# A two-layer hybrid decoder trunk: the order of output blocks and token chunks in three residual products, and how long their weights are kept

## The chip, the cores and the metric

The kernel runs on one core of one Trainium2 chip. The metric is the time of one execution on the device, in microseconds, and less is better. The engines are called as in the profile: PE multiplies matrices (PEld is its weight load), DVE, ACT and POOL are the three engines for elementwise work, and SP issues most of the transfers.

## What is computed

One inference step of two layers with 1024 features, for a prompt of 16 meta tokens and 512 tokens and for eight samples of 8 tokens, 592 tokens in all:

```
layer 0:  x = LN(a*x + W_out @ [stick-breaking attention | multi-scale pooling])
          x = LN(a*x + W_down @ (gelu(conv3(W_g x)) * (W_v x)))
layer 1:  x = LN(a*x + W_out @ (gelu(W_gate x) * RG-LRU(conv4(W_rec x))))
          x = LN(a*x + W_down @ (gelu(conv3(W_g x)) * (W_v x)))
```

a is the fourth root of 4, the FFN has 2816 hidden features, and RG-LRU is a gated linear recurrence along the tokens. LN takes the mean and the variance over the 1024 features of a token. The outputs are y without the meta tokens, and the caches (keys, values, pooling, convolution and recurrence states).

## The kernel before, in words

Features lie on the 128 partitions, tokens along the free dimension; 1024 features are eight blocks of 128. The tokens are cut into two chunks, chunk 0 (0 to 295) and chunk 1 (296 to 591). In the second half of layer 1 chunk 0 leaves out the first 14 tokens and has 282 columns.

**Products.** Every product is done in a split form of fp32. `split` (L100, L101) makes a high half on ACT and a low half, the difference, on DVE or POOL, and `mm3` (L127) then does three matmuls for each block of 128 inputs: high weight by high operand, high weight by low operand, low weight by high operand. `weights` loads one output block's weights over SP's queue into `wraw` and splits them into `whl`. `wraw` has two buffers, the split weights have six in layer 1 and in both FFNs (two pools in turn).

**Residual products.** The class `Residual` does a product whose result is added to the residual x (`r0_m` is block m of x for chunk 0, `r1_m` that for chunk 1) and the LayerNorm behind it. There are four: the attention's output, the last group of layer 0's FFN (6 input blocks, from about 731 us), the output of the recurrent layer (5 input blocks), and the last group of layer 1's FFN (6 input blocks, the end of the kernel). `mms(0)` does the eight output blocks of chunk 0 in the order 0 to 7, and keeps the weights of the last `keep` (3) blocks; then `second` does chunk 1 in the order 7 to 0 with `mms(1)`, which loads the weights of the other five again. Behind each block `post` adds it to x (L201), subtracts a first estimate of the mean (L209; the tile `s0` or `s1`, taken from the first block of that chunk at L206 to L207) and adds x and its square on POOL to the sums S1 (L219; a copy, L211, for the first block) and S2 (L220); "post" stands below for L201 and L209. The sums' tiles are `S10` and `S20` for chunk 0, `S11` and `S21` for chunk 1. `stats` lets PE sum S1 and S2 over the partitions with a matrix of ones (L228, tiles `mu` and `q2`), and takes the root of the variance on ACT (L232) with one refining step on DVE (L234 to L236). `norm` then centres each block (L250), scales it (L251), adds the bias (L252) and makes the high half `xh` on ACT (L257) and the low half `xl` on POOL (L258): the operands of the next stage. At the end of the kernel there is no next stage; the blocks go out, and POOL does four of chunk 1's eight normalisations and leaves two of its sums to PE.

**What sets the order.** The statistics and norms of a chunk are not done at once but put into a list, `pend`, and taken from it by `pop` between later pieces of PE work: those of chunk 0 while chunk 1's blocks are done, those of chunk 1 during the first blocks of the next stage. Each is given a high priority (`urgent`), so that the scheduler puts it ahead of other work on its engine. Each engine then works through its own list in order.

```
            for k, _ in enumerate(self.mms(1)):
                if k == 0:
                    self.pop()
                elif k >= 2:
                    self.pop(1 if k < 12 else 2)
```

**The next stages.** Layer 1 begins with five blocks on chunk 0 (three of the recurrent branch, tile `prc`, and two of the gate branch, `pgt`, 120 matmuls), then those blocks on chunk 1. A finished recurrent block goes through the convolution `conv4` (L937 and following, DVE), whose result is split (`ch`, `cl`) for the gate matrices (`pga`, L961) of the recurrence. An FFN begins with six blocks of W_g (tile `pg`) on chunk 0 and then on chunk 1.

## Time and profile before

| | |
|---|---|
| time, three executions | 1468.46, 1469.25, 1470.31 us (median 1469.25) |
| the profiled execution | 1470.56 us, span of the core 1468.8 us |
| PE busy | 1371.5 us, 93% of the span |
| DVE, ACT, POOL busy | 56%, 40%, 31% |
| chain of work that ended last | PE 75%, DVE 14%, issue 4%, ACT 3%, POOL 2% |
| weights loaded for the three products | 26 blocks of 384 KB (both FFNs), 13 of 320 KB (recurrent output) |

A row of the profile in order of time begins with the start and the length in us; x8 says that it stands for eight instructions in a row. What stands in brackets at its end is the idle time of that engine just before, and what ended it. A row of a group has the busy time in us and the mean ns of one instruction behind the bar.

### The profile page before, as it was taken

How to read it: one execution, taken by the hardware profiler on the slowest of the kernel's cores; microseconds unless marked ns; L12 is line 12 of the kernel's file. 1: busy time of each engine (PE TensorE's matmuls, PEld its weight loads, DVE VectorE, ACT ScalarE, POOL GpSimd, SP SyncE). 2: the span in 40 equal slices, each digit the busy share in tenths (PEclk: the TensorE clock that was granted, in tenths of full speed). 3: DMA queues.
4: the chain of work that ended last, by engine and by line, in shares of the span. 5: the costliest groups of instructions: out<-in, count | busy, mean ns of one | idle time of the engine just before them, and what ended most of it. 6: DMA issues, size and time to landing. Idle time of an engine off the chain costs nothing.

```text
span 1468.8 us, 26738 instructions
## 1 busy us (share of the span) xinstructions
PE 1371.5 (93%) x10491; PEld 1294.3 (88%) x10491; DVE 816.1 (56%) x1220; ACT 587.3 (40%) x1083; POOL 451.2 (31%) x621
## 2 busy tenths in 40 slices
PE   8999798998999999999997787897999999999995
PEld 7988555798999999999997787886999999999994
DVE  4226676575743344334477699888734344433456
ACT  4333575444522233213245466735522133312333
POOL 3112220346320011102257656447531012101244
PEclk9999899999999999999998898998999999999997
DMA  9499887842422222222241210143222222222121
GB/s 311 169 373 372 308 286 259 302 135 87 129 73 87 86 73 87 79 80 79 67 120 58 62 65 28 28 121 115 73 91 82 87 81 78 87 87 87 57 90 65
DMA packets 78592, 183.74 MB, mean 125 GB/s; under 512 B 9458, under 2 KB 18291, under 8 KB 78467
## 3 DMA queue, kind: packets, MB, share of 16 engines
q1 hardware_dynamic: 75362, 170.77, 35.3%
q0 software_dynamic: 3104, 11.27, 2.1%
q8 instruction: 83, 1.36, 0.4%
q14 instruction: 43, 0.34, 0.1%
HBM read 176.38 MB, written 5.62 MB: 124 GB/s over the span
## 4 chain that ended last, share of the span: by engine, by line
PE 75%; DVE 14%; issue 4%; ACT 3%; POOL 2%; DMA 1%; SPq 0%; DVEq 0%; ACTq 0%; POOLq 0%
PE pv L127 19%; PE pg L127 18%; PE pdn L127 14%; PE pr L127 4%; PE pqk L127 3%; PE zs L640 2%; PE pv L415 2%; DVE r L251 2%; PE av L668 2%; DVE whl L101 2%; PE zp L517 1%; PE pu L127 1%; DVE r L250 1%; PE prc L127 1%; DVE r L209 1%
## 5 line engine op out<-in xcount | busy, mean ns | idle before, releaser
L100 ACT ACTIVATE whl<-wraw 128x1024 fp32r<-128x1024 f32 (+4 forms) x217 | 212.4, 981 | 338.9 <-PE pdn L127 150.6
L127 PE MATMUL pg<-xh,whl 128*128 128x296 f32 (+1 forms) x1408 | 293.0, 300 | 4.2 <-ACT xh L257 4.2
L101 DVE TENSOR_TENSOR whl<-wraw,whl 128x1024 fp32r<-128x1024 f32 (+3 forms) x198 | 234.9, 1187 | 102.2 <-ACT whl L100 101.6
L127 PE MATMUL pv<-xh,whl 128*128 128x296 f32 (+1 forms) x1408 | 290.2, 298 | 0.0
L127 PEld LDWEIGHTS pg<-xh,whl 128*128 128x128 f32 x1408 | 231.5, 191 | 4.8 <-ACT xh L257 4.4
L127 PEld LDWEIGHTS pv<-xh,whl 128*128 128x128 f32 x1408 | 229.0, 188 | 0.0
L127 PE MATMUL pg<-xl,whl 128*128 128x296 f32 (+1 forms) x704 | 210.7, 301 | 6.8 <-POOL xl L258 6.8
L127 PE MATMUL pv<-xl,whl 128*128 128x296 f32 (+1 forms) x704 | 209.1, 297 | 0.0
L127 PE MATMUL pdn<-fh,whl 128*128 128x296 f32 (+1 forms) x1024 | 207.7, 298 | 0.0
L101 POOL TENSOR_TENSOR fl<-f,fh 128x592 fp32r<-128x592 f32 (+1 forms) x44 | 82.7, 1879 | 273.1 <-ACT fh L100 273.1
L127 PEld LDWEIGHTS pdn<-fh,whl 128*128 128x128 f32 x1024 | 165.5, 188 | 0.0
L127 PE MATMUL pdn<-fl,whl 128*128 128x296 f32 (+1 forms) x512 | 151.7, 297 | 0.0
L127 PEld LDWEIGHTS pg<-xl,whl 128*128 128x128 f32 x704 | 133.8, 191 | 9.0 <-POOL xl L258 8.9
L127 PEld LDWEIGHTS pv<-xl,whl 128*128 128x128 f32 x704 | 133.0, 189 | 0.0
L807 DVE TENSOR_SCALAR gc<-ge,sm 128x608 f32<-128x608 f32 x44 | 26.2, 595 | 169.4 <-ACT ge L770 159.4
L801 POOL COPY fout<-ge 128x2 f32<-128x2 f32 x44 | 15.7, 358 | 326.1 <-ACT ge L767 326.0
L767 ACT ACTIVATE ge<-pg 128x296 f32<-128x296 f32 (+2 forms) x88 | 33.8, 386 | 157.2 <-PE pg L127 155.2
L127 PEld LDWEIGHTS pdn<-fl,whl 128*128 128x128 f32 x512 | 96.4, 189 | 0.0
L393 DVE TENSOR_TENSOR_SCAN kp<-kp,zero 128x256 f32<-128x256 f32 (+5 forms) x70 | 54.1, 774 | 73.7 <-ACT kp L392 73.2
L864 DVE SCALAR_TENSOR_TENSOR r<-r,pdn 128x296 f32<-128x296 f32 (+1 forms) x64 | 29.0, 459 | 118.0 <-PE pdn L127 118.0
L821 DVE TENSOR_TENSOR f<-gc,pv 128x296 f32<-128x296 f32 (+1 forms) x88 | 37.5, 426 | 99.6 <-PE pv L127 75.4
L127 PE MATMUL pr<-fh,whl 128*128 128x296 f32 (+1 forms) x384 | 79.4, 300 | 0.0
(263 smaller groups left out, 2726.9 us busy)
## 6 DMA issues: line engine op xcount, KB each, us to landing
ck<-in_ck SPq DMA_DIRECT2D x128, 256.0 KB, 5.1
cv<-in_cv SPq DMA_DIRECT2D x128, 256.0 KB, 5.2
wraw<-in_w_g SPq DMA_DIRECT2D x44, 512.0 KB, 3.3
wraw<-in_w_vv SPq DMA_DIRECT2D x44, 512.0 KB, 3.4
wraw<-in_w_d SPq DMA_DIRECT2D x32, 512.0 KB, 3.3
wraw<-in_w_d SPq DMA_DIRECT2D x26, 384.0 KB, 3.1
wraw<-in_w_lo SPq DMA_DIRECT2D x13, 320.0 KB, 3.0
wraw<-in_w_o POOLq DMA_DIRECT2D x8, 512.0 KB, 6.4
```

What stands on the lines that cost most here:

```text
L100: act.activation(h, src, AF.Copy)
L101: (le or dve).tensor_tensor(l, src, h.bitcast(F32), op=OP.subtract)
L127: pe.matmul(ps, lhsT=w[:, wi, s], rhs=x[k][:, lo:hi], start=(n == 0), stop=(n == 3 * nk - 1))
L251: dve.scalar_tensor_tensor(x, x, g, rs, op0=OP.mult, op1=OP.mult)
L393: dve.tensor_tensor_scan(kp[:, n - 1::-1], kp[:, n - 1::-1], zero.to_broadcast([128, n]), 1.0 if carry is None else carry, op0=OP.mult, op ...
L415: pe.matmul(p, lhsT=x[k][:, i * 128:i * 128 + n], rhs=w[k // 4][:, wi, s], start=(j == 0), stop=(j == 3 * KB - 1))
L640: pe.matmul(z[c * 32:c * 32 + 32, :256].rearrange("p (j n) -> p j n", j=2), lhsT=qb[b][:, c, r, :], rhs=kt[:, b, :, c * 128:c * 128 + 128] ...
L668: pe.matmul(av[c * 32:c * 32 + 32], lhsT=an[:, j * 128 + c * 32:j * 128 + c * 32 + 32], rhs=vt[:, :, j, c * 128:c * 128 + 128], start=(u = ...
L767: act.activation(e[:, k + lo:k + z], p[:, :z - lo], AF.Copy)
L807: dve.tensor_scalar(t[:, :n], e[:, :n], cws[0], smc("fcb", L * FB + j), op0=OP.mult, op1=OP.add)
L821: dve.tensor_tensor(f[:, lo:z], t[:, lo:z], p[:, :z - lo], op=OP.mult)
L864: dve.scalar_tensor_tensor(x, x, ALPHA if gi == 0 else 1.0, p, op0=OP.mult, op1=OP.add)
```

## The change

Three of the four residual products no longer call `mms(0)` and `second`, but a new method `both(4)`. It does output blocks 0 to 3 for both chunks in turn (chunk 0, then chunk 1), then blocks 4 to 7 for chunk 0, then 7 to 4 for chunk 1. A block's weights are kept until both chunks have used them, so each is loaded and split once: 16 blocks of 384 KB instead of 26, and 8 of 320 KB instead of 13. The statistics and norms of chunk 0 are put on the list behind its last block and taken from it in eight steps between the halves of chunk 1's last four blocks (1, 1, 2, 2, 1, 1, 1, 1 entries); what is left goes to the next stage. The last lines of `mms` become a method `finish`, and the attention's product stays as it was.

```
--- before.py
+++ after.py
@@ -44,6 +44,7 @@
 STEP = 3.5
 HQ, EP = 19, 8
 PRO = 6
+JOINT = 4
 WINDOWS = (2, 4, 8, 16)
 CTX = 15
 BW = 3 + TP + NS * 11
@@ -187,6 +188,38 @@
                     prev()
                 prev = partial(self.post, ci, m, p, n)
                 yield 0.19 * nk, 0.09 * nk
+            self.finish(ci, prev)
+
+        def both(self, nj):
+            nk, ws, prev = self.nk, {}, None
+            seen = [0, 0]
+            seq = [(m, ci) for m in range(nj) for ci in range(2)] + [(m, 0) for m in range(nj, KB)]
+            seq += [(m, 1) for m in range(KB - 1, nj - 1, -1)]
+            late = deque()
+            for m, ci in seq:
+                lo, hi = self.chunks[ci]
+                if m not in ws:
+                    ws[m] = weights(self.wsrc[m], nk)
+                p = psum["d"]("pr")[:, :hi - lo]
+                for k in (0, nk // 2):
+                    mm3(p, ws[m], self.ih, self.il, lo, hi, nk, k, nk // 2 if k == 0 else nk)
+                    if seen[0] == KB:
+                        self.pop(late.popleft())
+                if prev is not None:
+                    prev()
+                prev = partial(self.post, ci, m, p, seen[ci])
+                seen[ci] += 1
+                if ci:
+                    del ws[m]
+                if (m, ci) == (KB - 1, 0):
+                    late.extend([1, 1, 2, 2] + [1] * (2 * (KB - nj) - 4))
+                    self.finish(0, prev)
+                    prev = None
+            self.finish(1, prev)
+
+        def finish(self, ci, prev):
             self.pend.append(prev)
             self.pend.append(partial(self.urgent, HPS, self.stats, ci))
             for m in range(KB):
@@ -865,9 +898,7 @@
             else:
                 sp.dma_start(O["ffn"][:, L], fout)
                 res = Residual(I[f"w_d{gi}"][L], nk, hh, hl, 1.0, 2 * L + 1, last, chunks)
-                for _ in res.mms(0):
-                    pass
-                res.second()
+                res.both(JOINT)
         return res
 
     res.second()
@@ -1044,9 +1075,7 @@
     a, b = LGROUPS[1]
     res = Residual(I["w_lo1"], b - a, [ys[i][0] for i in range(a, b)], [ys[i][1] for i in range(a, b)], 1.0, 2,
                    chunks=CH2)
-    for _ in res.mms(0):
-        pass
-    res.second()
+    res.both(JOINT)
     res = ffn(1, res, True)
     res.pop(99)
 
```

Lines behind the new code have other numbers: L128, L242, L252, L253, L284 and L290 of the changed kernel are L127, L209, L219, L220, L251 and L257 of the one before.

POOL, in layer 0's FFN product, from chunk 0's first sum on. Before (the tiles are chunk 0's sums `S10`, `S20`, its blocks `r0_m` and their squares `sq0`):

```order
L211 COPY S10_8418<-r0_0_78 128x296
L220 TENSOR_TENSOR S20_8419<-S20_8419,sq0_8452 128x296
L219 TENSOR_TENSOR S10_8418<-S10_8418,r0_1_79 128x296
L220 TENSOR_TENSOR S20_8419<-S20_8419,sq0_8482 128x296
L219 TENSOR_TENSOR S10_8418<-S10_8418,r0_2_80 128x296
L220 TENSOR_TENSOR S20_8419<-S20_8419,sq0_8512 128x296
```

and in the changed kernel, where `S11`, `S21`, `r1_m` and `sq1` are those of chunk 1:

```order
L244 COPY S10_8413<-r0_0_78 128x296
L244 COPY S11_8447<-r1_0_4146 128x296
L252 TENSOR_TENSOR S10_8413<-S10_8413,r0_1_79 128x296
L253 TENSOR_TENSOR S20_8414<-S20_8414,sq0_8476 128x296
L253 TENSOR_TENSOR S21_8448<-S21_8448,sq1_8506 128x296
L252 TENSOR_TENSOR S11_8447<-S11_8447,r1_1_4147 128x296
L252 TENSOR_TENSOR S10_8413<-S10_8413,r0_2_80 128x296
L253 TENSOR_TENSOR S20_8414<-S20_8414,sq0_8531 128x296
L252 TENSOR_TENSOR S11_8447<-S11_8447,r1_2_4148 128x296
```

Chunk 0's sums now take turns with chunk 1's, for the first four blocks of each.

DVE, from the last scaling of chunk 0 to the first centring of chunk 1, behind the same product. Before (`pr` is a block's product, `whl` the split weights of layer 1's first blocks, `s1` the mean of chunk 1):

```order
L251 SCALAR_TENSOR_TENSOR r0_7_85<-r0_7_85,sm_70,S10_8418 128x296
L201 SCALAR_TENSOR_TENSOR r1_1_4147<-r1_1_4147,pr_8848 128x296
L101 TENSOR_TENSOR whl_9091<-wraw_9090,whl_9091 128x1024
L201 SCALAR_TENSOR_TENSOR r1_0_4146<-r1_0_4146,pr_8878 128x296
L209 TENSOR_TENSOR r1_1_4147<-r1_1_4147,s1_8679 128x296
L101 TENSOR_TENSOR whl_9128<-wraw_9127,whl_9128 128x1024
L209 TENSOR_TENSOR r1_0_4146<-r1_0_4146,s1_8679 128x296
L250 TENSOR_TENSOR r1_0_4146<-r1_0_4146,s1_8679 128x296
```

and in the changed kernel:

```order
L284 SCALAR_TENSOR_TENSOR r0_6_84<-r0_6_84,sm_70,S10_8413 128x296
L284 SCALAR_TENSOR_TENSOR r0_7_85<-r0_7_85,sm_70,S10_8413 128x296
L283 TENSOR_TENSOR r1_0_4146<-r1_0_4146,s1_8446 128x296
L283 TENSOR_TENSOR r1_2_4148<-r1_2_4148,s1_8446 128x296
L283 TENSOR_TENSOR r1_1_4147<-r1_1_4147,s1_8446 128x296
L283 TENSOR_TENSOR r1_4_4150<-r1_4_4150,s1_8446 128x296
```

Chunk 1's last two posts and two weight splits now stand ahead of chunk 0's scalings, and the centring of chunk 1 follows the scalings directly.

ACT, the last high halves of chunk 0 (`xh5` to `xh7`) there, the mean of chunk 1 (L229, L230) and the root of its variance (L232). Before:

```order
L257 ACTIVATE xh5_8658<-r0_5_83 128x296
L100 ACTIVATE whl_9356<-wraw_9355 128x1024
L257 ACTIVATE xh6_8659<-r0_6_84 128x296
L257 ACTIVATE xh7_8660<-r0_7_85 128x296
L229 ACTIVATE S11_8680<-mu_8995 128x296
L230 ACTIVATE s1_8679<-mu_8995 128x296
L232 ACTIVATE S11_8680<-S21_8681 128x296
L767 ACTIVATE re0_8973<-prc_8942 128x296
L767 ACTIVATE re1_9024<-prc_8982 128x296
```

and in the changed kernel, where the root is L265 and the bias of chunk 1's first block is L285:

```order
L290 ACTIVATE xh3_8750<-r0_3_81 128x296
L290 ACTIVATE xh4_8751<-r0_4_82 128x296
L290 ACTIVATE xh5_8752<-r0_5_83 128x296
L265 ACTIVATE S11_8447<-S21_8448 128x296
L290 ACTIVATE xh6_8753<-r0_6_84 128x296
L290 ACTIVATE xh7_8754<-r0_7_85 128x296
L285 ACTIVATE r1_0_4146<-r1_0_4146,sm_70 128x296
```

The root of chunk 1 now stands ahead of the last two high halves of chunk 0.

PE, in layer 1, the first blocks on chunk 1 (`prc` with different numbers are different recurrent blocks, `pgt` is a gate block). Before:

```order
L127 MATMUL prc_9161<-xh0_8653,whl_8938 128x296
L127 MATMUL prc_9201<-xh0_8653,whl_8978 128x296
L127 MATMUL prc_9241<-xh0_8653,whl_9128 128x296
L127 MATMUL pgt_9281<-xh0_8653,whl_9039 128x296
L127 MATMUL prc_9161<-xl0_8661,whl_8938 128x296
L127 MATMUL prc_9161<-xh0_8653,whl_8938 128x296
L127 MATMUL prc_9201<-xl0_8661,whl_8978 128x296
L127 MATMUL prc_9201<-xh0_8653,whl_8978 128x296
```

and in the changed kernel, at the end of the first recurrent block and the begin of the second:

```order
L128 MATMUL prc_9136<-xh6_8753,whl_8913 128x296
L128 MATMUL prc_9136<-xh7_8754,whl_8913 128x296
L128 MATMUL prc_9136<-xl7_8762,whl_8913 128x296
L128 MATMUL prc_9136<-xh7_8754,whl_8913 128x296
L128 MATMUL prc_9176<-xh0_8747,whl_8953 128x296
L128 MATMUL prc_9176<-xl0_8755,whl_8953 128x296
L128 MATMUL prc_9176<-xh0_8747,whl_8953 128x296
```

Before, four blocks took turns at each operand; now a block goes through all eight operands before the next one begins.

## Rows read from the trace of the kernel before

**Rows 1.** The page's busy times, over the whole span.

```profile
PE 1371.5 (93%) x10491; PEld 1294.3 (88%) x10491; DVE 816.1 (56%) x1220; ACT 587.3 (40%) x1083; POOL 451.2 (31%) x621
```

**Rows 2.** Windows: busy time (and instructions) by engine, granted clock, DMA share, GB/s.

```profile
730.70:770.40 39.70, 38.52 (x275) 37.81 (x275) 28.27 (x50) 17.29 (x29) 20.06 (x18) 1.00 0.38 111
770.40:830.00 59.60, 43.88 (x265) 41.62 (x264) 43.91 (x51) 27.59 (x62) 43.71 (x42) 0.83 0.17 55
820.00:900.00 80.00, 61.55 (x393) 59.41 (x394) 75.64 (x66) 51.26 (x80) 49.90 (x43) 0.87 0.19 63
1009.00:1060.00 51.00, 44.16 (x302) 42.80 (x302) 40.97 (x55) 30.53 (x69) 36.88 (x38) 0.90 0.25 79
1445.00:1469.00 24.00, 6.29 (x12) 3.88 (x12) 12.76 (x22) 8.43 (x18) 9.82 (x11) 0.64 0.25 86
```

**Rows 3.** Waits of PE, 765 to 832 us: total, times, longest.

```profile
PE prc L127 <- ACT xh L257: 6.2, 2, 3.2
PE pga L961 <- ACT ch L100: 6.8, 1, 6.8
```

**Rows 4.** Groups by form on DVE, whole span: weight splits by width.

```profile
L101 DVE TENSOR_TENSOR whl<-wraw,whl 128x1024 fp32r<-128x1024 f32 x154 | 191.9, 1246 | 85.4 <-ACT whl L100 85.1
...
L101 DVE TENSOR_TENSOR whl<-wraw,whl 128x768 fp32r<-128x768 f32 x26 | 27.5, 1056 | 6.5 <-ACT whl L100 6.2
...
L101 DVE TENSOR_TENSOR whl<-wraw,whl 128x640 fp32r<-128x640 f32 x13 | 13.2, 1012 | 7.8 <-ACT whl L100 7.8
```

**Rows 5.** Groups by form on POOL, 740 to 760 us: the sums of chunk 0.

```profile
L219 POOL TENSOR_TENSOR S<-S,r 128x296 f32<-128x296 f32 x7 | 8.4, 1196 | 0.0
L220 POOL TENSOR_TENSOR S<-S,sq 128x296 f32<-128x296 f32 x7 | 7.5, 1077 | 0.9 <-ACT sq L215 0.9
```

**Rows 6.** POOL in order of time: the last sum of chunk 0 there.

```profile
757.42 1.52 POOL L219 TENSOR_TENSOR S<-S,r 128x296 f32<-128x296 f32 x1
```

**Rows 7.** PE in order of time: chunk 0's statistics, first and second chunk of layer 1.

```profile
758.99 0.77 PE L228 MATMUL mu<-S,ones 128*128 128x296 f32 x2 [1.18 <-POOL S L219]
...
776.62 0.62 PE L127 MATMUL prc<-xh,whl 128*128 128x296 f32 x1 [3.01 <-ACT xh L257]
...
803.06 1.06 PE L127 MATMUL prc<-xh,whl 128*128 128x296 f32 x3 [3.24 <-ACT xh L257]
...
824.86 1.36 PE L961 MATMUL pga<-ch,wga 128*128 128x296 f32 x4 [6.79 <-ACT ch L100]
```

**Rows 8.** DVE in order of time, from chunk 0's statistics to layer 1's first convolution.

```profile
760.75 3.10 DVE L250 TENSOR_TENSOR r<-r,s 128x296 f32<-128x296 f32 x8
...
773.59 8.07 DVE L251 SCALAR_TENSOR_TENSOR r<-r,sm,S 128x296 f32<-128x296 f32 x8
...
791.66 6.59 DVE L250 TENSOR_TENSOR r<-r,s 128x296 f32<-128x296 f32 x8 [5.34 <-ACT s L230]
...
800.71 4.72 DVE L251 SCALAR_TENSOR_TENSOR r<-r,sm,S 128x296 f32<-128x296 f32 x8
...
815.06 0.60 DVE L937 TENSOR_SCALAR rt<-re,sm 128x616 f32<-128x616 f32 x1 [9.63 <-ACT re L770]
```

**Rows 9.** ACT in order of time: the last two operands of chunk 0.

```profile
788.06 0.78 ACT L257 ACTIVATE xh<-r 128x296 fp32r<-128x296 f32 x2
```

**Rows 10.** The chain of waits behind the recurrent output product: start us, us, what.

```profile
1030.67 28.35 PE pg L127 x209
```

**Rows 11.** DVE in order of time, behind the recurrent output product.

```profile
1010.58 6.96 DVE L251 SCALAR_TENSOR_TENSOR r<-r,sm,S 128x282 f32<-128x282 f32 x8
```

**Rows 12.** POOL in order of time, same place.

```profile
1026.67 3.94 POOL L258 TENSOR_TENSOR xl<-r,xh 128x282 fp32r<-128x282 f32 x4
```

**Rows 13.** The end of the kernel, DVE in order of time.

```profile
1440.93 5.75 DVE L251 SCALAR_TENSOR_TENSOR r<-r,sm,S 128x282 f32<-128x282 f32 x8
...
1455.32 0.47 DVE L231 SCALAR_TENSOR_TENSOR S<-q,S 128x296 f32<-128x296 f32 x1 [6.15 <-PE q L228]
...
1460.05 0.47 DVE L236 SCALAR_TENSOR_TENSOR S<-sq,S 128x296 f32<-128x296 f32 x1
```

## The prediction

> **What bounds the kernel now.** I read the page's busy times first. TensorE (PE) is busy for 1371.5 of 1468.8 us [rows 1], so the kernel is PE's, and only what makes PE wait, or wait less, can move the end. The windows then say where it waits [rows 2]. The product of layer 0's FFN that this change reorders runs from 730.7 to 770.4 us with PE busy for 38.52 of 39.70 us: it is full, although it reloads five weights. The loss lies right behind the products: 43.88 busy of 59.60 us from 770.4, 44.16 of 51 us from 1009, and 6.29 of the last 24 us. There PE waits for normalised tokens, or the kernel for its last ones. Between 820 and 900 us it is another engine: VectorE (DVE) is busy for 75.64 of 80 us, PE for 61.55. The list of PE's waits behind layer 0's product names the operand h of the next stage, 6.2 us in two waits, and the gate matrices of layer 1, which wait 6.8 us for the first convolution's result [rows 3]. So the change is worth what it moves in the LayerNorms behind the three products, not what it saves in loading.
>
> **The reloads themselves: nothing directly.** Each product loads eight weights instead of thirteen. On DVE that takes away ten splits of 768 columns at 1.056 us and five of 640 at 1.012 us, 15.6 us in all [rows 4]; ScalarE (ACT) loses their high halves and SP's queue their loads, so that the next stage's weights come sooner; with a DMA share of 0.38 [rows 2] they were not late. Inside the products PE was full, so I cost this at 0. It counts only where DVE is behind.
>
> **Place 1, behind layer 0's FFN product.** Times are on the clock of the execution before.
>
> (a) Chunk 0's statistics come later. Its eighth block is now the twelfth on PE, and POOL sums the blocks of both chunks as they come. Ahead of chunk 0's last sum of x there stood one copy and 13 sums; now two copies and 18. Sums take 1.196 and 1.077 us [rows 5], 1.14 on the mean, so five more and a copy (taken as 0.6, half a sum) are 6.3 us. Before, the last sum ended at 757.42 + 1.52 = 758.94 us [rows 6] and the matmul for the mean followed at 758.99 [rows 7]; now it is ready at 765.2. In PE's order the matmul stands behind 251 of the product's 288; at 39.70/288 = 0.138 us each that is 730.7 + 34.6 = 765.3 us. The two meet, so PE hardly waits for it.
>
> (b) Chunk 0's normalising. From that matmul DVE needed 14.6 us before it began the eight scalings of L251 at 773.59 [rows 8]: 1.8 us until it could start and 12.8 us full of centring (L250), three weight splits, and posts of chunk 1. Now one split (1.25 us, [rows 4]) and five small operations at 0.47 us fewer stand there, which leaves 9.2 us; but POOL is still summing, and eight centrings then take up to 6.59 us instead of 3.10 [rows 8]. I take half of that 3.5 us more: 765.4 + 1.8 + 9.2 + 1.7 = 778 us, 4.5 us later than before.
>
> (c) Chunk 1 comes earlier. Before, four posts and two splits stood between the two chunks, then DVE waited 5.34 us for chunk 1's mean, because POOL was still summing. Now its sums are done when DVE gets there, and the centring follows at once: 778 + 8.07 + 6.59 = 792.7 us, and scaling 2.5 us after that (798.25 to 800.71 before), at 795.2 us instead of 800.71 [rows 8].
>
> (d) PE. ACT's order now has chunk 1's root ahead of the last two operands of chunk 0, so these come at about 794 us instead of 788.06 [rows 9], and their low halves by 795.5. Of the 120 matmuls on chunk 0, 55 stand behind the last of these: at 28.35/209 = 0.136 us, as in the row of the other transition [rows 10], they end at 803 us. Chunk 1 began at 803.06 [rows 7]: no gain for PE here. But chunk 1 is then ready as a whole, and PE does its first recurrent block at one go, 24 matmuls or 3.3 us, where it took turns between four blocks. DVE's first convolution can begin at about 806.5 instead of 815.06 us, where it stood idle for 9.63 us [rows 8]. The gate matmuls stand behind four such blocks, 803 + 13.1 = 816 instead of 824.86, with their operand long there. From here DVE bounds the layer [rows 2], and its work is the same. **Term 1: 8.5 us gained.** If only PE counted it would be 0; if POOL left DVE alone, see the third rival, 14.
>
> **Place 2, behind the recurrent output product.** The same pattern: by (a) and (b) chunk 0's scaling begins some 3.5 us later than 1010.58 and takes the same 6.96 us [rows 11], to 1021. POOL no longer has sums of chunk 1 between the low halves, which then follow each other: the last six, at 3.94/4 = 0.985 us, end at 1027.4 instead of 1030.6 us [rows 12]. From there PE was full [rows 10], and so it stays; PE's order has three matmuls more ahead of the last low half (77 instead of 74), 0.4 us. **Term 2: 3.2 + 0.4 = 3.6 us.** Ends: 0 and 7.
>
> **Place 3, the end.** DVE did chunk 0's eight scalings from 1440.93, 5.75 us, ahead of the last three blocks of chunk 1; so chunk 1's statistics reached it only at 1455.32 [rows 13]. Now the scalings begin some 6 us later, 1447, but chunk 1's last sums and products are all ahead of them. They end at 1452.7, and chunk 1's variance follows at once, 2.6 us earlier. From there the end is taken as the same; the second half of the centring, which falls on a DVE at work until 1460.05 [rows 13], may gain or lose a little. **Term 3: 2.6 us.** Ends: 0, if the scalings slip to 1449.6 and so end at 1455.3 as before, and 6, the wait of 6.15 us in that row.
>
> **The sum:** 8.5 + 3.6 + 2.6 = 14.7 us. The profiled execution took 1470.56 us around its span of 1468.8, 1.3 us above the median 1469.25. So 1470.6 - 14.7 - 1.3 = 1454.6 us for a median. What a measurement of this kernel can tell from no change is about 0.2%, 2.9 us.
>
> **A rule weighed.** Eight centrings took 3.10 us with POOL idle and 6.59 us with POOL at work, eight scalings 8.07 and 4.72 [rows 8]: a DVE operation there takes about as long as the POOL operation that it runs beside. The Trainium skill, "SBUF — State Buffer", section "SBUF: two separate sides", says that DVE operations with two SBUF inputs and GpSimd operations exclude each other for the whole instruction. The trace agrees. By that rule the added sums stretch beside DVE and the total is at worst the first rival's, 1476 us; were the two engines free of each other, it would be the third's, 1448 us.
>
> **The rivals.**
> 1. *Slower: POOL becomes the bound.* Chunk 0's statistics wait for 19 sums in each of the three places. The mean was 1.14 us, but a sum beside DVE took 1.52 [rows 6]. If all do, each place loses 19 x 0.38 = 7.2 us: terms of 1.3, -3.6 and -4.6, together 6.9 us slower, 1476 us. It decides from a mean of 1.14 + 14.7/57 = 1.40 us. For it: the sums lie in a row with no idle time. Against it: with five fewer splits DVE disturbs POOL less. Chance 0.10.
> 2. *Layer 1 follows PE, not DVE.* Term 1 is then 0 and 6.2 us remain: 1463.1 us. For it: PE's start of chunk 1 does not move, and it has 61.55 us of work in the 80 of [rows 2]. Against it: DVE has 75.64. Chance 0.20.
> 3. *DVE undisturbed.* POOL's sums end before the scalings begin; then these take 4.72 us and the centrings 3.10 [rows 8], 6.8 us less. Chunk 0's operands come that much earlier and PE ends chunk 0 some 5.5 us earlier: term 1 is 14, term 2 about 5, term 3 as it was, 21.6 us in all: 1447.7 us. For it: chunk 1's sums are done sooner. Against it: the low halves keep POOL at work. Chance 0.13.
> 4. *No change.* Chunk 0's delay of 4.5 us costs PE at both places what chunk 1's earliness gives back: terms 0, -3.5 and 2.6, about 1470 us. For it: no wait that PE shows is for a reload. Against it: chunk 1's operands are there as a whole. Chance 0.10.
>
> **The numbers.** The forecast has 0.47: 1454.6. Its own bounds, some 4.5 us either way for the share of contention in (b), are 1450 to 1459; with rivals 2 and 3 and 2 to 3 us around each they give 1446 to 1466. This leaves out rivals 1 and 4, 0.20. Faster: 0.47 + 0.20 + 0.13 = 0.80; same, rival 4, 0.10; slower, rival 1, 0.10.
>
> **What would show it.** Weight splits of 768 and 640 columns on DVE at 16 and 8. Right, if DVE's first convolution starts near 806 us and PE's wait of 6.8 us for the gates' operand is gone; if the last low half of place 2 ends near 1027, less what was gained; if chunk 1's variance at the end follows L251 without a gap. Wrong, if PE stands idle inside a product ahead of the matmul of chunk 0's mean, or if DVE's first convolution starts early and the layer ends no earlier.

## The result, and the profile after

| | before | changed kernel |
|---|---|---|
| median | 1469.78 us (4 executions) | 1454.71 us (1453.72 to 1459.36, 4 executions) |
| ratio to before | | 0.9897, 95% interval 0.9877 to 0.9916 |
| the profiled execution, span | 1470.56, 1468.8 us | 1454.59, 1452.8 us |

The kernel is 15.1 us faster (12 to 18 by the interval); 1454.6 was forecast. The forecast's size was right. At place 1 the events came as forecast, up to the gate matrices; what carries the gains to the end was given wrongly (places 1 and 2) or left out in part (the clock, place 3).

Lines of the changed kernel are named by their own numbers (L283 centring, L284 scaling, L291 low half, L261 statistics). The clearest comparison is by stretches, cut where the reordered products start: the first product's start to that of the recurrent output product (place 1), from there to the next FFN's first down product (place 2), the FFN, and the last product's start to the end (place 3). First the windows of the kernel before (length, then PE, PEld, DVE, ACT and POOL busy, granted clock, DMA share, GB/s):

```profile
730.66:969.00 238.34, 198.60 (x1310) 191.09 (x1309) 201.09 (x229) 137.01 (x232) 140.28 (x146) 0.92 0.21 62
969.00:1122.79 153.79, 143.19 (x1022) 140.39 (x1021) 100.62 (x153) 68.67 (x128) 74.49 (x75) 0.96 0.31 98
1122.79:1404.50 281.71, 281.71 (x2115) 281.71 (x2113) 110.37 (x160) 74.45 (x114) 36.27 (x68) 1.00 0.25 81
1404.50:1468.80 64.30, 46.71 (x310) 43.65 (x308) 44.08 (x74) 25.78 (x50) 34.09 (x35) 0.87 0.23 74
```

and those of the changed kernel:

```profile
731.11:958.98 227.87, 196.51 (x1310) 189.31 (x1309) 197.69 (x224) 133.04 (x227) 139.68 (x146) 0.93 0.18 56
958.98:1110.44 151.46, 140.16 (x1022) 137.96 (x1021) 98.11 (x149) 65.12 (x123) 64.63 (x75) 0.97 0.28 89
1110.44:1392.52 282.08, 282.08 (x2114) 282.08 (x2113) 110.39 (x160) 74.46 (x114) 36.97 (x68) 1.00 0.25 80
1392.52:1452.80 60.28, 44.15 (x310) 41.73 (x308) 36.26 (x69) 21.45 (x45) 31.77 (x35) 0.88 0.14 46
```

Place 1 gives 10.47 us, place 2 gives 2.33, place 3 gives 4.02, and the FFN between takes 0.37 back: 16.45 us together. The spans differ by 16.0, because the first product began 0.45 us later. Of a stretch, what PE lost has two parts: its idle time (length less busy), and busy time at the lower clock. For the second, I took windows of 1 us and added up busy time x (1 - granted clock):

| | idle before, after | lost to the clock before, after |
|---|---|---|
| place 1 | 39.7, 31.4 us | 13.7, 12.4 us |
| place 2 | 10.6, 11.3 us | 4.5, 2.1 us |
| place 3 | 17.6, 16.1 us | 3.0, 0 us |

So at place 1 PE waits less, and at the other two it works less at half the clock (1.2 instead of 2.4 GHz). The runs below agree where a place has the same code: the old order loses 4.5 to 7.0 us to the clock at place 2 (four runs) and 2.7 to 3.0 at place 3 (three runs), the new one 1.6 to 2.7 (four runs) and 0 (six runs).

DVE in order of time behind the first product of the changed kernel, the rows that answer to [rows 8]:

```profile
768.12 2.85 DVE L283 TENSOR_TENSOR r<-r,s 128x296 f32<-128x296 f32 x4
771.27 1.58 DVE L283 TENSOR_TENSOR r<-r,s 128x296 f32<-128x296 f32 x4
...
777.79 8.93 DVE L284 SCALAR_TENSOR_TENSOR r<-r,sm,S 128x296 f32<-128x296 f32 x8
786.64 5.62 DVE L283 TENSOR_TENSOR r<-r,s 128x296 f32<-128x296 f32 x8
...
795.71 5.32 DVE L284 SCALAR_TENSOR_TENSOR r<-r,sm,S 128x296 f32<-128x296 f32 x8
...
806.97 0.60 DVE L968 TENSOR_SCALAR rt<-re,sm 128x616 f32<-128x616 f32 x1 [5.93 <-ACT re L803]
```

and PE there, against [rows 7] (chunk 0's mean, the last matmul on chunk 0 together with the first on chunk 1, the gate matrices):

```profile
766.36 0.66 PE L261 MATMUL mu<-S,ones 128*128 128x296 f32 x2
...
802.84 0.43 PE L128 MATMUL prc<-xh,whl 128*128 128x296 f32 x2
...
816.08 0.71 PE L992 MATMUL pga<-ch,wga 128*128 128x296 f32 x4
```

Chunk 1 begins with the second of the two matmuls at 802.84, at 802.98: that is 120 block matmuls behind the first on chunk 0 (781.18), and its first block is done 24 matmuls later, when ACT takes it up:

```profile
806.45 0.36 ACT L800 ACTIVATE re<-prc 128x232 f32<-128x232 f32 x1 [0.86 <-PE prc L128]
```

None of the three rows of PE has idle time in front of it: the brackets of [rows 7], 3.24 us for an operand of chunk 1 and 6.79 us for the gates' operand, are gone. The waits of PE, 765 to 832 us, against [rows 3] (total, times, longest):

```profile
PE mu L261 <- POOL S L252: 7.9, 1, 7.9
PE pga L992 <- ACT wga L101: 3.9, 1, 3.9
PE prc L128 <- ACT gt L957: 1.0, 1, 1.0
```

Two long waits are left. That for a split gate matrix comes later, at 829.55 us (in the kernel before it was 1.18 us, at 836.97). The other is for chunk 1's sums of x at 780.46 us; but chunk 0's first operand was ready no sooner than 780.65 (ACT writes it from 780.22, 0.43 us), and PE began on it at 781.18, so this wait costs some 0.5 us. These starts cut place 1 into four:

| | before | changed kernel |
|---|---|---|
| to the first matmul on chunk 0 | 45.96 us | 50.07 us |
| the blocks on chunk 0 | 26.44 us | 21.80 us |
| four blocks on chunk 1, to the gates | 21.80 us | 13.10 us |
| from the gates on | 144.14 us | 142.90 us |

So 9.2 of the 10.5 us are there when the gates begin, 8.7 of them in the four blocks on chunk 1, which run without a wait (6.8 us before) and at the full clock (1.7 us lost before). The rest of the layer takes nearly as long as before. Weight splits on DVE are down as the order says:

```profile
L102 DVE TENSOR_TENSOR whl<-wraw,whl 128x768 fp32r<-128x768 f32 x16 | 15.7, 983 | 2.4 <-ACT whl L101 2.4
L102 DVE TENSOR_TENSOR whl<-wraw,whl 128x640 fp32r<-128x640 f32 x8 | 6.6, 820 | 4.0 <-ACT whl L101 4.0
```

### The profile page after: what moved, and what is told of

Same layout as the page of the kernel before. It is cut to its first block, busy times and chain, and to the rows that moved or that the text cites. A ratio compares the mean times of both kernels' runs of the same rounds, so it can differ in the third digit from the quotient of the medians.

```text
span 1452.8 us, 26627 instructions
## 1 busy us (share of the span) xinstructions
PE 1365.2 (94%) x10491; PEld 1288.9 (89%) x10491; DVE 802.6 (55%) x1205; ACT 575.7 (40%) x1067; POOL 439.4 (30%) x621
## 3 DMA queue, kind: packets, MB, share of 16 engines
q1 hardware_dynamic: 73202, 165.19, 34.4%
## 4 chain that ended last, share of the span: by engine, by line
PE 78%; DVE 12%; issue 4%; ACT 3%; POOL 2%; DMA 1%; SPq 0%; DVEq 0%; ACTq 0%; POOLq 0%
PE pv L128 20%; PE pg L128 19%; PE pdn L128 14%; PE pr L128 8%; PE pqk L128 4%; PE zs L673 2%; PE av L701 2%; PE pv L448 2%; DVE r L283 2%; PE zp L550 1%; PE pu L128 1%; DVE whl L102 1%; DVE r L284 1%; DVE aa L1000 1%; PE op L570 1%
## 5 line engine op out<-in xcount | busy, mean ns | idle before, releaser
L101 ACT ACTIVATE whl<-wraw 128x1024 fp32r<-128x1024 f32 (+4 forms) x202 | 200.5, 993 | 331.0 <-PE pdn L128 150.6
L128 PE MATMUL pg<-xh,whl 128*128 128x296 f32 (+1 forms) x1408 | 291.7, 299 | 0.3 <-ACT xh L290 0.3
L128 PE MATMUL pv<-xh,whl 128*128 128x296 f32 (+1 forms) x1408 | 290.4, 298 | 0.0
L102 DVE TENSOR_TENSOR whl<-wraw,whl 128x1024 fp32r<-128x1024 f32 (+3 forms) x183 | 219.2, 1198 | 94.4 <-ACT whl L101 93.7
L128 PEld LDWEIGHTS pg<-xh,whl 128*128 128x128 f32 x1408 | 230.5, 190 | 1.3 <-ACT xh L290 1.1
L128 PEld LDWEIGHTS pv<-xh,whl 128*128 128x128 f32 x1408 | 228.8, 188 | 0.0
L128 PE MATMUL pg<-xl,whl 128*128 128x296 f32 (+1 forms) x704 | 209.0, 299 | 4.0 <-POOL xl L291 4.0
L128 PE MATMUL pv<-xl,whl 128*128 128x296 f32 (+1 forms) x704 | 208.9, 297 | 0.0
L128 PE MATMUL pdn<-fh,whl 128*128 128x296 f32 (+1 forms) x1024 | 207.7, 297 | 0.0
L128 PEld LDWEIGHTS pdn<-fh,whl 128*128 128x128 f32 x1024 | 165.4, 188 | 0.0
L128 PE MATMUL pdn<-fl,whl 128*128 128x296 f32 (+1 forms) x512 | 151.5, 297 | 0.0
L128 PEld LDWEIGHTS pg<-xl,whl 128*128 128x128 f32 x704 | 133.0, 189 | 5.3 <-POOL xl L291 5.2
L128 PEld LDWEIGHTS pv<-xl,whl 128*128 128x128 f32 x704 | 132.8, 189 | 0.0
L834 POOL COPY fout<-ge 128x2 f32<-128x2 f32 x44 | 10.5, 240 | 337.3 <-ACT ge L800 337.2
L128 PEld LDWEIGHTS pdn<-fl,whl 128*128 128x128 f32 x512 | 96.3, 188 | 0.0
L128 PE MATMUL pr<-fh,whl 128*128 128x296 f32 (+1 forms) x384 | 79.9, 301 | 0.0
```

What stands on the lines that cost most here:

```text
L101: act.activation(h, src, AF.Copy)
L102: (le or dve).tensor_tensor(l, src, h.bitcast(F32), op=OP.subtract)
L128: pe.matmul(ps, lhsT=w[:, wi, s], rhs=x[k][:, lo:hi], start=(n == 0), stop=(n == 3 * nk - 1))
```

## The experiments

The stretch "behind the first product" below is a run's span less the start of its first reordered product: 738.14 us before, 721.69 us changed. It is used beside the timed ratios because the code ahead of it is the same in all kernels but one (sums_on_pe), and yet the product began anywhere from 728.5 to 734.8 us in the profiled executions. Each stretch comes from one profiled execution.

### One place at a time

```
# p1_place1: layer 0's FFN alone (the recurrent output goes back to mms(0) and second)
-                res.both(JOINT)
+                if not last:
+                    res.both(JOINT)
+                else:
+                    for _ in res.mms(0):
+                        pass
+                    res.second()
# p2_place2: the recurrent output alone; p3_place3: "if last" in the FFN alone, and
#            the recurrent output back as in p1_place1
```

Expected of p1_place1:

> The new order at layer 0's FFN product alone. Theory: the gain sits behind the products, mostly here; the prediction's term 1 is 8.5 us, and the starts of the recurrent output product in the two traces (969.00 and 958.98 us, the first product starting at 730.66 and 731.11) say 10.5. So 8.5 to 10.5 us below the kernel before, 1459 to 1461 us. Rival (layer 1 follows PE, not DVE): 0 to 2 us. Rival (the gain is the saved loads, the same at each place by their number): 10 of 25 reloads are 768 wide and in two products, 5 here, so about 5 us.

Of p2_place2:

> The new order at the recurrent output product alone. Prediction's term 2: 3.6 us gained. By the traces (from the start of that product to the first down product of the next FFN 153.79 us before, 151.46 now) 2.3 us. So 1466 to 1468 us. Rival (the gain is the saved loads): about 5 us.

Of p3_place3:

> The new order at the last product alone. Prediction's term 3: 2.6 us gained. By the traces (from the start of the last product to the end 64.3 us before, 60.3 now) 4.0 us: 1465 to 1467 us. Rival (the gain is the saved loads): about 5 us. If the three places add up, the gains of the three runs together are the 15 us of the whole change.

Measured: ratios to before 0.9925 (0.9904 to 0.9947), 0.9980 (0.9964 to 0.9996) and 0.9968 (0.9954 to 0.9983), that is 11, 3 and 5 us. The changed stretch of each, by windows:

```profile
732.25:960.08 227.83, 195.43 (x1310) 188.25 (x1309) 197.79 (x224) 132.82 (x227) 139.77 (x146) 0.93 0.17 56
...
969.92:1120.74 150.82, 139.92 (x1022) 137.69 (x1021) 97.22 (x148) 65.67 (x123) 63.88 (x75) 0.97 0.26 89
...
1403.47:1463.60 60.13, 44.14 (x310) 41.72 (x308) 36.25 (x69) 21.46 (x45) 31.83 (x35) 0.89 0.14 47
```

Place 1 alone takes 10.5 us less than before, place 2 alone 3.0 and place 3 alone 4.2. Each is near what the whole change shows at that place, so the three add up to nearly the whole (17.7 and 16.8 us at the three places; by the ratios 19 and 15 us, with some 4 us either way). An equal gain of 5 us at each place, for five saved loads each, is ruled out by place 1. (The change saves 15 loads, not the 25 of the expectation.)

### The order without the saved loads

```
-                if m not in ws:
+                if m not in ws or (ci and m <= nj):
```

> The new order of blocks and chunks at all three places, but blocks 0 to 4 are loaded and split again for chunk 1, so that each product loads 13 blocks as before. Theory (the order gives the gain, the saved loads nothing directly): 0 to 3 us above the changed kernel, since one more split stands ahead of chunk 0's scalings: 1454 to 1458 us. Rival (the saved loads and splits give it): the gain is gone, 1467 to 1470 us.

Measured: 0.9924 (0.9904 to 0.9943), by the ratios some 4 us above the changed kernel, with intervals that overlap a little. Behind the first product 728.71 us, 7.0 more than the changed kernel and 9.4 less than before: 2.65 more at place 1, 4.19 at place 2, 0.18 at place 3. The rival falls, and the theory holds only in part: the order gives more than half, but the loads are not free. At place 2 they take back the whole gain: 155.65 us, where the new order took 150.63 to 152.05 us in four runs and the old one 153.55 to 155.20. The waits of PE there, 960 to 1015 us of this run:

```profile
PE mu L261 <- POOL S L252: 12.2, 2, 9.2
PE sh L239 <- DVE r L234: 0.9, 1, 0.9
```

and PE in order of time, inside the product:

```profile
993.19 0.30 PE L128 MATMUL pr<-yl,whl 128*128 128x296 f32 x1
996.47 1.31 PE L261 MATMUL mu<-S,ones 128*128 128x282 f32 x2 [2.97 <-POOL S L252]
997.17 1.10 PE L128 MATMUL pr<-yh,whl 128*128 128x296 f32 x2
998.06 0.45 PE L128 MATMUL pr<-yl,whl 128*128 128x296 f32 x1
```

DVE's splits push back its posts (DVE no longer waits for PE's blocks there, as it does in the changed kernel), these POOL's sums, and the matmul of chunk 0's mean comes 34.4 us behind the product's start instead of 31.1. PE's first operand of the next stage then comes at 51.2 us instead of 48.1, which is most of the 4.19. PE waits 2.97 us for the mean, and a matmul behind it takes 0.45 instead of 0.30 us: the clock has fallen, and two windows of 4 us show it at 0.67 and 0.50 on PE:

```profile
994.00:998.00 4.00, 1.53 (x4) 1.27 (x5) 3.29 (x6) 2.67 (x4) 4.00 (x4) 0.67 0.00 0
998.00:1002.00 4.00, 4.00 (x17) 3.73 (x16) 4.00 (x5) 3.48 (x6) 4.00 (x5) 0.50 0.51 180
```

This is the price of the loads in the new order. No run has the old order with fewer loads.

### Fewer or more blocks in turn

```
-JOINT = 4
+JOINT = 3          # joint2: 2; joint5: 5, and:
-                    late.extend([1, 1, 2, 2] + [1] * (2 * (KB - nj) - 4))
+                    late.extend([1, 1] + [2] * (2 * (KB - nj) - 2))
```

Expected of joint3:

> Three output blocks in turn instead of four, five blocks' weights kept. Theory: behind the recurrent output product and at the end PE now waits only for chunk 0's first operands (place 2: first matmul of the next stage 48.1 us behind the start of the product), and chunk 0's statistics come one piece of PE work (about 2 us) earlier; behind layer 0's product chunk 1's operands decide. So place 2 gains 1 to 2 us, places 1 and 3 stay: 1452 to 1455 us. Rival (chunk 1's statistics being early is what gives the gain everywhere, chunk 1 now standing later relative to chunk 0's norms): 2 to 4 us slower than the changed kernel, 1457 to 1459 us.

Of joint2:

> Two output blocks in turn, six blocks' weights kept, which is every buffer there is. Theory: place 2 gains 2 to 4 us by chunk 0's earlier statistics, if the next stage's weights, which now wait for buffers, are there in time; places 1 and 3 lose up to 2 us as chunk 1's work moves nearer to chunk 0's norms: 1451 to 1456 us. Rival (buffers decide): the first matmuls of the next stage wait for weights, 1458 us or more.

Of joint5:

> Five output blocks in turn, three blocks' weights kept; chunk 0's norms are taken from the list in six steps (1, 1, 2, 2, 2, 2). With two and three in turn place 1 took 2.8 and 2.2 us more than with four, place 3 1.4 and 1.8. If the trend goes on (chunk 1's earliness decides): 1452 to 1454 us. Rival (chunk 0's delay decides from here on, its statistics come another 2 us later): 1456 to 1458 us.

Measured: 0.9914 (0.9898 to 0.9929), 0.9910 (0.9893 to 0.9926) and 0.9877 (0.9851 to 0.9903) for two, three and five. Place 1 takes 230.65, 230.08, 227.87 and 226.00 us with two to five, place 2 takes 151.42, 152.67, 151.46 and 150.71, and place 3 takes 61.67, 62.07, 60.28 and 61.07. One and the same code took 150.63 to 152.05 us at place 2 and 60.13 to 61.29 at place 3 in these runs, so only place 1 speaks clearly. The expected gain at place 2 from an earlier chunk 0 did not come. At place 1 the time falls with each block done in turn, and does not flatten: the gates come 89.2, 86.6, 85.0 and 82.8 us behind the product's start with two to five. With two, PE waits 4.22 us for the gates' operand again. This points to chunk 1's earliness, as chunk 0 comes later with each block; joint5 also takes chunk 0's norms from the list in larger steps. By the timed ratios none of the three can be told from the changed kernel.

### POOL's sums beside DVE

```
-            if self.last and ci == 1 and n >= KB - NR:
+            if ci == 1 and n >= KB - NR:
```

> The changed kernel, and the last two blocks of chunk 1 are summed by PE in the statistics of all three places (now only in the last), which takes four sums off POOL at each of places 1 and 2, and adds four matmuls to PE, some 1.3 us. Theory (POOL beside DVE stretches chunk 0's scalings, 8.93 us there against 3.47 at the end of the kernel, where POOL is idle): the scalings of place 1 take 6 to 7 us, those of place 2 4 us or less, and chunk 1's mean comes 2 to 4 us earlier: 2 to 4 us faster than the changed kernel, 1451 to 1453 us. Rival (the weight splits and low halves stretch them, not the sums): no change or 1 to 2 us slower for the added matmuls.

The edit reaches the attention's product too, which lies ahead of the three places; what it costs there is not shown.

Measured: 0.9895 (0.9877 to 0.9913), no different from the changed kernel. But the places differ: 225.03 us at place 1 (2.8 less), 156.19 at place 2 (4.7 more). At place 1 the theory holds; DVE in order of time there, chunk 0's scalings:

```profile
778.71 6.83 DVE L284 SCALAR_TENSOR_TENSOR r<-r,sm,S 128x296 f32<-128x296 f32 x8
```

6.83 us instead of 8.93, with four sums fewer on POOL. At the end of the changed kernel eight scalings, of 282 instead of 296 columns, take 3.47 us. POOL has nothing to do there until 1437.55 us, and its first operation then takes 2.38 us, where each of the next three takes 1.03:

```profile
1435.79 3.47 DVE L284 SCALAR_TENSOR_TENSOR r<-r,sm,S 128x282 f32<-128x282 f32 x8
```

```profile
1437.55 5.35 POOL L279 TENSOR_TENSOR r<-r,s 128x296 f32<-128x296 f32 x4 [6.86 <-ACT s L263]
```

At place 2 the scalings are shorter too (3.47 us instead of 4.45), but PE gets its first operand no sooner, 48.9 us behind the product's start (48.1 in the changed kernel), and what follows takes 3.9 us more. Most of that is clock. Windows of this run, around and behind that operand:

```profile
1005.00:1009.00 4.00, 2.17 (x7) 1.84 (x8) 3.87 (x9) 4.00 (x12) 3.04 (x2) 0.50 0.00 0
1009.00:1013.00 4.00, 4.00 (x19) 4.00 (x18) 3.13 (x4) 2.05 (x7) 4.00 (x5) 0.50 0.01 4
1013.00:1017.00 4.00, 4.00 (x26) 4.00 (x26) 4.00 (x6) 2.77 (x7) 3.67 (x5) 0.78 0.00 0
```

and the changed kernel at its first operand, which came at 1007.06:

```profile
1003.00:1007.00 4.00, 2.34 (x4) 1.01 (x4) 3.93 (x7) 1.27 (x4) 2.39 (x3) 0.50 0.46 146
1007.00:1011.00 4.00, 3.94 (x24) 3.94 (x25) 4.00 (x9) 4.00 (x12) 2.08 (x3) 0.77 0.00 0
```

Behind the first operand PE lost 3.98 us to the clock here and 0.88 in the changed kernel, counted as in the table above, and it waited another 0.89 us for a low half. In the changed kernel PE works from the statistics at 1004.46 us on with one break of 0.26 us; here it has pauses around its first operand (2.17 us busy of four), and it works at the lower clock for longer.

### What bounds layer 1

```
# dve_dose
+        dve.tensor_scalar(t[:, :n], t[:, :n], 1.0, 0.0, op0=OP.mult, op1=OP.add)
         xc = blk(f"xc{i}")
# pe_dose
         p = pd("pgt", hi - lo)
+        for _ in range(6 if i > 1 else 0):
+            pe.matmul(p, lhsT=w[:, 0, :128], rhs=xh[0][:, lo:hi], start=True, stop=True)
```

Expected of dve_dose:

> The changed kernel with one more DVE operation of 616 columns, about 0.6 us, in each of the eight convolutions of layer 1 (times one, plus zero). Theory (DVE bounds layer 1 behind place 1, as the prediction's term 1 assumed): 8 x 0.6 = 4.8 us and up to 8 us where POOL stretches them, 1459 to 1463 us. Rival (PE bounds it, and the layer came earlier because PE did): 0 to 1 us, 1455 to 1456 us.

Of pe_dose:

> The changed kernel with six more matmuls ahead of each chunk of a gate block 2 to 7 in layer 1, 72 in all, 72 x 0.136 = 9.8 us of PE work at the full clock; their result is overwritten by the block's own first matmul. DVE's added work cost nothing in the run before, so it does not bound layer 1 by its busy time. Rival of the prediction's term 1 (PE bounds the layer): 8 to 10 us slower than the changed kernel, 1463 to 1465 us. Other theory (a chain across the engines sets the pace behind the first convolution, PE has 17 us idle and 9.5 us lost to the lower clock between 830 and 959 us): 0 to 4 us, 1455 to 1459 us, and part of the idle time is gone.

Measured: dve_dose 0.9878 (0.9861 to 0.9894), no slower than the changed kernel, and place 1 takes 226.86 us instead of 227.87. The windows of the changed kernel and of dve_dose, 820 to 940 us:

```profile
820.00:940.00 120.00, 99.00 (x637) 95.15 (x636) 111.69 (x106) 83.53 (x131) 66.33 (x66) 0.90 0.15 46
```

```profile
820.00:940.00 120.00, 97.78 (x637) 94.13 (x636) 115.68 (x113) 83.62 (x132) 70.94 (x68) 0.93 0.14 46
```

DVE is busy 4 us more, and nothing is later. A busy time of 111.69 of 120 us was therefore not a full DVE. The pe_dose run has 0.9919 (0.9898 to 0.9940), by the ratios 3 us above the changed kernel, which the intervals do not separate. Its place 1:

```profile
734.77:968.62 233.85, 203.93 (x1382) 197.64 (x1381) 200.00 (x224) 131.28 (x225) 141.89 (x146) 0.94 0.16 55
```

72 matmuls more, PE busy for 7.42 us more, and the stretch 5.98 us longer, all of it behind the gates (148.88 us instead of 142.90; 141.81 in dve_dose). So of 9.8 us of added work six arrive. Of the other four, PE lost 2.1 us less to the clock behind the gates (7.5 instead of 9.7 us; p1_place1, with the same code as the changed kernel there, lost 8.5) and was idle 1.1 us less. It lies between the two theories: PE's own work is part of the pace of layer 1, not all of it.

### The clock by itself

```
# on the kernel before
                 res.second()
+                if last:
+                    wm = pd("wm", T - CW)
+                    for r in range(8):
+                        pe.matmul(wm, lhsT=ones, rhs=hh[r % nk].bitcast(F32)[:, CW:], start=r == 0, stop=r == 7)
```

> The kernel before, with eight matmuls of matrices of ones (some 4 us at the full clock) behind the last product, where PE stood idle for 3.98 us ahead of chunk 1's statistics; their result is not used. Theory (3 of the 4 us that the change gained at the end are the clock: the twelve statistics matmuls ran at half the clock behind that idle time, 1448.90 to 1455.18 us, and at the full one in the changed kernel): the statistics take 3.2 instead of 6.3 us and the kernel gets 2 to 3 us faster than before. Rival (the gain comes from the order of DVE's work alone, the clock is a bystander): no change, or up to 1 us slower for the added work.

Measured: 0.9987 (0.9971 to 1.0002), which the timing alone does not tell from no change. The traces do. The window of chunk 1's statistics in the kernel before, and that in this run (six matmuls each; the profile has each of these fp32 matmuls twice, x12):

```profile
1448.90:1455.18 6.28, 6.28 (x12) 3.88 (x12) 0.27 (x1) 1.17 (x3) 1.08 (x2) 0.51 0.00 0
```

```profile
1450.04:1453.28 3.24, 3.24 (x12) 2.12 (x12) 0.27 (x1) 0.90 (x3) 0.94 (x1) 1.00 0.00 0
```

The same matmuls take 3.24 us instead of 6.28, at a granted clock of 1.00 instead of 0.51. PE in order of time shows what it did ahead of them (x16 for the eight of the edit):

```profile
1445.88 4.15 PE L874 MATMUL wm<-fh,ones 128*128 128x296 f32 x16
1450.04 0.77 PE L228 MATMUL mu<-S,ones 128*128 128x296 f32 x2
```

The last stretch took 61.78 instead of 64.30 us (64.12 and 64.15 in p1_place1 and p2_place2, which have the old code there), with no change in the order of anything. So 2.5 us of the end's gain can be had by the clock alone. The Trainium skill, "TensorE: Matmul & The Clock Gate", section "HAM oscillation — how this bites in real kernels", says that a pause of PE lets its clock fall to the half, and counts the cost as the extra time of the work done at it. The trace agrees: 6.28 and 3.24 us for one and the same work.

### Put together

The changed kernel, with the sums of chunk 1's last two blocks on PE at place 1 and the end, and 16 matmuls of ones in PE's idle time at place 2:

```
-            if self.last and ci == 1 and n >= KB - NR:
+            if (self.last or self.ln == 1) and ci == 1 and n >= KB - NR:
...
     res.both(JOINT)
+    wm = pd("wm", T - CW)
+    for r in range(16):
+        pe.matmul(wm, lhsT=ones, rhs=res.ih[r % res.nk].bitcast(F32)[:, CW:], start=r == 0, stop=r == 15)
```

> The changed kernel, with the last two blocks of chunk 1 summed by PE at place 1 (2.8 us gained there in the run with PE's sums at all places, 4.7 lost at place 2 to a lower clock) and with sixteen matmuls of ones, some 8 us, in PE's idle time between the recurrent output product and chunk 1's statistics, whose result is not used. Theory: place 1 takes 225 us instead of 227.9, and at place 2 the 2 us that PE lost to the lower clock are gained back: 1449.5 to 1452 us. Rival (the added matmuls are in the way of chunk 1's statistics, or the clock falls all the same): 1452 to 1454 us.

Measured: 0.9875 (0.9853 to 0.9897). Behind the first product 719.02 us, 2.7 less than the changed kernel, which the timing can't tell from it. The clock at place 2 stays at 1.00 as hoped:

```profile
960.54:1111.17 150.63, 146.85 (x1054) 142.81 (x1053) 98.38 (x148) 65.02 (x123) 63.77 (x75) 1.00 0.26 90
```

but the place is only 0.8 us shorter, which lies within what the same code took in other runs. Place 1 took 225.96 us, 1.9 less. Most of the 2 us was lost in the statistics (1.2 us, against 0.9 behind them), ahead of an operand that PE had to wait for anyway; this part of the theory falls.

## Why the prediction was right, and where its reasons were not

Times behind a product's start compare the executions: 730.66, 969.00 and 1404.50 us before, 731.11, 958.98 and 1392.52 in the changed kernel. Other times are on the clock of their own execution.

- **The reloads, costed at 0: wrong, above all at place 2.** "Inside the products PE was full" was read from layer 0's product and taken over to the recurrent output's, where it does not hold: with the same order and the old loads chunk 0's mean and the next stage's first operand came 3 us later, and 4.2 us were lost there, 2.65 at place 1. Shown by order_only. The clause that loads count where DVE is behind was right, but the place was not looked for. The trace of the kernel before already has PE idle inside that product, ahead of the matmul of chunk 0's mean:

```profile
994.39 1.31 PE L228 MATMUL mu<-S,ones 128*128 128x282 f32 x2 [2.02 <-POOL S L219]
```

- **Place 1 (a) to (c): right.** Chunk 0's mean was put 34.7 us behind the product's start and came at 35.25. The scaling of chunk 0 was put at 778 and came at 777.79, the end of chunk 1's centring at 792.7 and came at 792.26, its scaling at 795.2 and came at 795.71.
- **Place 1 (d): events right, what follows them wrong.** Chunk 0's last two operands came at 793.80 (about 794 forecast) and their low halves at 795.36 (795.5), chunk 1 began at 802.98 (803), DVE's first convolution at 806.97 (806.5) and the gates at 816.08 (816). But "from here DVE bounds the layer, and its work is the same" falls with dve_dose. From the gates on the layer took 142.90 us, 142.81 in p1_place1 and 141.81 in dve_dose, against 144.14 before: it ends earlier because it begins earlier, and what sets its pace is only in part PE's work (pe_dose). The term came out at 10.5 instead of 8.5 us, 9.2 at the gates and 1.2 behind them. In PE's time its idle time fell by 8.4 us and its loss to the clock by 1.3.
- **Place 2: the event right, the bound wrong.** The last low half was to come 3.2 us earlier and came 3.7 earlier (57.9 us behind the product's start against 61.6), though chunk 0's scaling began 4.2 us later (3.5 forecast) and took 4.45 instead of 6.96 us (taken as the same). But PE no longer waited for this low half: from its first operand on PE was full, and this operand came 3.9 us later than before. PE in order of time, before:

```profile
1013.18 1.55 PE L127 MATMUL pg<-xh,whl 128*128 128x282 f32 x5 [4.17 <-ACT xh L257]
1016.86 0.60 PE L127 MATMUL pg<-xl,whl 128*128 128x282 f32 x1 [2.12 <-POOL xl L258]
```

  and in the changed kernel:

```profile
1007.06 1.78 PE L128 MATMUL pg<-xh,whl 128*128 128x282 f32 x6 [0.26 <-ACT xh L290]
```

  What pays is the stretch behind this operand, 6.2 us shorter: PE neither waits there (2.7 us before) nor works long at the lower clock (2.9 us lost before, 0.9 now), and chunk 1's statistics now lie ahead of it, which is most of the other 1.5. The term was 2.3 instead of 3.6 us.
- **Place 3: the order right, the clock missed.** The scalings began 6.8 us later (6 forecast) and were expected to keep their 5.75 us; they took 3.47. Chunk 1's variance followed them at once:

```profile
1439.18 0.46 DVE L264 SCALAR_TENSOR_TENSOR S<-q,S 128x296 f32<-128x296 f32 x1
```

  That is 46.66 us behind the product's start instead of 50.82, 4.2 us earlier where 2.6 were forecast. The forecast left out that before, PE's pause of 3.98 us was followed by statistics at half the clock. PE loses 3.0 us less to the clock by the table, and warm_end had 2.5 of the 4.0 us in the old order by the clock alone. The two gains do not add: in the changed kernel PE's statistics end at 1437.23, 1.95 us before the variance, and the scalings decide.
- **The rivals.** POOL as the bound (1): no. POOL's 22 sums of both chunks had a mean of 1.05 us:

```profile
L253 POOL TENSOR_TENSOR S<-S,sq 128x296 f32<-128x296 f32 x11 | 12.4, 1133 | 0.0
L252 POOL TENSOR_TENSOR S<-S,r 128x296 f32<-128x296 f32 x11 | 10.7, 974 | 1.5 <-DVE r L242 1.5
```

  Layer 1 following PE (2): what spoke for it held, as PE's start of chunk 1 hardly moved (71.9 us behind the product's start, 72.4 before), but its price was wrong, as PE's wait of 6.79 us ahead of the gates went all the same. DVE undisturbed (3): at the end (3.47 us) and in part at place 2 (4.45); at place 1 chunk 0's scalings were disturbed more than ever (8.93). No change (4): no.

The sum came out right in part by luck: against the traces, term 1 was 2.0 us too low, term 3 1.4 too low and term 2 1.3 too high. The terms also put the loads at nothing, but for a split or two between DVE's operations; with the loads kept, the order gave 9.4 of the 16.45 us (by the ratios 11 of 15). That the medians met the forecast to 0.1 us says little, with an interval 6 us wide.

## What to carry to other kernels

When PE waits, ask what it does right behind the wait: work that trickles in at the lower clock costs double (6.28 us for 3.24 above), and one pause that is followed by a full run can be cheaper than two short ones. A stage's busiest engine is not its bound if its operations stretch beside another engine's: double one operation on it and look, before a term is built on it. Cut the profile into stretches at the change's own places and compare those, when the time ahead of them varies by more than the effect.

## What was not expected of the hardware

- A DVE at 93% of a stretch took 4 us more work in 120 us without any delay (111.69 and 115.68 us busy).
- In one execution eight scalings took 8.93 us beside POOL's sums, low halves and a weight split, and at the end 3.47 us (of 282 instead of 296 columns), where POOL began an operation only halfway and took 2.38 instead of 1.03 us for it. The Trainium skill, "SBUF — State Buffer", section "SBUF: two separate sides", has DVE operations with two SBUF inputs and POOL's operations exclude each other; the trace agrees, and taking four sums off POOL gave 2.1 us of the 8.93 back.
- Shorter scalings at place 2, with four sums moved from POOL to PE, made the kernel slower there by 4.7 us, mostly through the clock: 3.98 instead of 0.88 us lost behind the first operand. The rest is a wait of 0.9 us and an operand that came 0.8 us later.

Not settled: what besides PE's work paces layer 1 behind the gates, where PE is idle for 21.8 of 142.90 us. DVE's 4 us cost nothing, six of the ten us that were added to PE arrived, and ACT and POOL were not tried there.
